# Latent attention with operands stored as two parts, softmax weights divided on ScalarE, linear attention scaled out of PSUM

## The chip, the core and the metric

One core of a Trainium2 chip runs the whole program. Its engines are TensorE (PE, with its weight loads PEld), VectorE (DVE), ScalarE (ACT), GpSimd (POOL), and SyncE (SP), which here only issues DMAs. The metric is device microseconds for one execution, from the first to the last instruction and a little around it; lower is better.

## The reference, cut to what matters

The model has two layers on a sequence of 1024 tokens with 1024 features. The change lies in the mixer of the first layer, which feeds two heads' groups from one projection:

```
q  = rmsnorm(c_q, g_q) @ w_uq          # 8 heads of 64 + 32 rotary features
kv = rmsnorm(c_kv, g_kv) @ w_ukv       # 8 heads of 64 key + 64 value features
s  = (q_nope . k_nope + rope(q_pe) . rope(k_pe)) * 96 ** -0.5, causal
a  = softmax(s) @ v                    # latent attention, f32
o  = linear attention(gq, gk, gv, decay)        # 4 heads, chunks of the sequence
g  = rmsnorm(o, g_gla) * silu(r)
mix = concat(a, g) @ w_out
```

All of it is f32. A product of two f32 operands is made on TensorE from rounded parts: x = hi + lo, and hi.hi + hi.lo + lo.hi are three matmuls into the same PSUM bank.

## The kernel before, in words

A tile framework records the program and orders each engine's instructions by its own estimate; semaphores are set by it. Within an engine the order is then fixed. Four pools matter here. `u` has 34 buffers of 4 KB a partition for nearly everything in SBUF; `t2` has 3 buffers of 128x512; PSUM has `p1` with 4 banks and `p2` with 2 buffers of two banks. A tile waits for the last reader of the buffer's former tile, and that reader can be a store to DRAM. Each DMA of the SP queue counts on one of eight semaphores in turn (DMAHW0 to 7) and waits for the former DMA on its semaphore, so that at most eight are under way.

`split` (L134 to L143) makes the two parts: ACT copies x to hi with rounding (L137), DVE subtracts hi from x for lo (L143; POOL where `lo_eng` says so). `acc3` (L145 to L151) issues the three matmuls.

`mix0` (from L881) goes through these stages, with the microseconds of the trace:

- 14 to 205: input projections, gates, the latents and their norms; then for two groups of four heads the up-projection. `uq` makes rotary and plain queries, `uk` keys, the loop over `V` values. ACT copies queries and values out of PSUM (L1207, L1220, L1234), DVE copies keys (L1223). DVE multiplies the rotary queries by cosine and sine (L1210, L1211), POOL adds (L1212). The results go to DRAM by head as f32: `mq`, `mk`, `mkr`, `mv`.
- 205 to 250: the gate r of the linear attention, eight token blocks `tok` (L1151 to L1153) of 24 matmuls each. `silu` (L393 to L400) takes each out of PSUM with DVE, three passes on ACT, DVE; POOL multiplies by the gain `ggla` (L1245), and SP stores it to `grd` (L1246). With three `t2` buffers, a block's silu needs the store of the block two before it.
- 258 to 587: 32 steps, eight heads by four row pairs, in a hand-written order. In each step `scores` (L1276) multiplies queries by keys, DVE takes the row maximum (L1302), ACT the exponential with its sum (L1304), DVE the reciprocal (L1305) and the division of the weights (L1306). `values` of two steps before and `turn` of the step before follow: `turn` transposes the weights on PE (L1319) and splits them. Every fourth step `head_qk` loads the next head's query and key to a raw tile and splits them into parts, 96x1024 each; every eighth `pair_v` does that for two heads' values. Between the steps run the linear attention `gla` (L930), one chunk of 128 tokens after the other, and `mem_side`, which prepares the cross attention and whose POOL splits (L143) read two 128x1024 tiles.
- `gla` makes decay factors `lev` (POOL L961, ACT L962, DVE L963), products `gr` on PE (L927, L976) that DVE copies under a mask (L977), and the chunk's output `o`, which sits in a `p2` buffer. ACT squares `o` (L1036), DVE multiplies `o` by the gate (L1037) and sums the squares (L1038), POOL makes the reciprocal root `stg` (L187, L188), DVE scales the four heads (L1042), PE transposes (L1048).

Of the kernel before, what the change touches and what calls it, by code (L numbers as in the profile page):

```python
# [7 lines left out]
F32 = mybir.dt.float32  # L8
# [7 lines left out]
P = 128  # L16
# [61 lines left out]
class Trunk:  # L78
# [802 lines left out]
    def mix0(self):  # L881
# [10 lines left out]
        wg, reset = c0[:, 0:256], c0[:, 256:384]  # L892
        ggla = self.cp.tile([P, P], F32, name="ggla")
        nc.sync.dma_start(ggla, self.bcast_row(T["g_gla"]))
        ones = self.cp.tile([P, P], F32, name="ones")
# [4 lines left out]

        qd, kd = self.dram("mq", [8, 96, S]), self.dram("mk", [8, 64, S])
        krd, vd = self.dram("mkr", [32, S]), self.dram("mv", [4, P, NT, P])

# [6 lines left out]
        def heads(x):  # L910
            return x.rearrange("p r (a b) -> p r a b", b=P)

        def natural(x):

            return x.rearrange("p (a r b) -> p r a b", a=2, b=P)

# [13 lines left out]
        def gla():  # L930
# [6 lines left out]
            for c in range(NT):  # L937
# [98 lines left out]
                nc.scalar.activation(at, o[:, :, 0:256], AF.Square, scale=128.0 ** -0.5)  # L1036
                nc.vector.tensor_tensor(natural(oc), heads(o[:, :, 0:256]), natural(srg), ALU.mult)  # L1037
                nc.vector.tensor_reduce(stt[:, 0:4], at.rearrange("p r (a b) -> p (r a) b", b=P), AX.X, ALU.add)  # L1038
                self.rstd(stt[:, 4:8], stt[:, 0:4])
                for hd in range(4):  # L1040
                    w, x = slice(hd * P, (hd + 1) * P), 4 + 2 * (hd % 2) + hd // 2
                    nc.vector.tensor_scalar(oc[:, w], oc[:, w], stt[:, x:x + 1], None, ALU.mult)  # L1042

                def turn(c=c, oc=oc):
                    tp = self.p1("gT")
                    for hd in range(4):
                        w = slice(hd * P, (hd + 1) * P)
                        nc.tensor.transpose(tp[:, w], oc[:, w], self.ident)  # L1048
# [13 lines left out]
        def head_qk(hd):  # L1062
            res = []
            for a in range(2):
                t = self.raw([P, S], "qk")
                if a:
                    nc.sync.dma_start(t[0:64, :], kd[hd])
                    nc.sync.dma_start(t[64:96, :], krd)
                else:
                    nc.sync.dma_start(t[0:96, :], qd[hd])  # L1070
                h, l = self.parts([96, S], "kq"[1 - a])
                self.split(h, l, t[0:96, :])
                res.append((h, l))
            qk[hd] = res

        def pair_v(pair):
            t = self.raw([P, NT, P], "V")
            nc.sync.dma_start(t.rearrange("p a b -> p (a b)"), vd[pair].rearrange("p a b -> p (a b)"))

            V[pair] = [self.u([P, NT, 2, 64], F32R, "V") for _ in range(2)]  # L1080
            for b, x in enumerate(V[pair]):
                self.split(x[:, :, 0, :], x[:, :, 1, :], t[:, :, 64 * b:64 * b + 64])


        with self.psum(4, 2):
# [55 lines left out]
            nc.gpsimd.tensor_tensor(kr[0:32, :], pe[0:32, :], kr[0:32, :], ALU.add)  # L1141
            nc.sync.dma_start(krd, kr[0:32, :])
            del pe, kr, wg, reset, c0

# [51 lines left out]
            for grp in range(2):  # L1196
                wuq = self.fetch(T["w_uq"][grp])

                def uq(t, half):
                    ps = self.p1("uq")  # L1200
                    self.acc3(ps, [(tuple(w[:, t * 256 + k * P:t * 256 + k * P + P] for w in wuq), tuple(x[:, half_cols(half)] for x in qn[k])) for k in range(2)])
                    return ps


                x, y = self.u([P, S], F32, "qpe"), self.u([P, S], F32, "swap")
                for half in range(2):
                    nc.scalar.activation(x[:, half_cols(half)], uq(0, half), AF.Copy, scale=asc)  # L1207
# [5 lines left out]
                for h in range(4):  # L1213
                    nc.sync.dma_start(qd[4 * grp + h, 64:96, :], x[32 * h:32 * h + 32, :])
                for pair in range(2 * grp, 2 * grp + 2):
                    q, k = self.u([P, S], F32, "q"), self.u([P, S], F32, "k")
                    w = slice(pair * P, pair * P + P)
                    for half in range(2):
                        c = half_cols(half)
                        nc.scalar.activation(q[:, c], uq(1 + pair % 2, half), AF.Copy, scale=asc)  # L1220
# [3 lines left out]
                    for b in range(2):  # L1224
                        nc.sync.dma_start(qd[2 * pair + b, 0:64, :], q[64 * b:64 * b + 64, :])
                        nc.sync.dma_start(kd[2 * pair + b], k[64 * b:64 * b + 64, :])
                w = slice(512 + grp * 256, 512 + grp * 256 + 256)
                for i in range(NT):
                    if not i % 4:
                        v = self.u([P, 4, 2, P], F32, "v")  # L1230
# [3 lines left out]
                    nc.scalar.activation(v[:, i % 4], ps[:, :256].rearrange("p (a b) -> p a b", a=2), AF.Copy)  # L1234
                    if i % 4 == 3:
                        for a in range(2):
                            nc.sync.dma_start(vd[2 * grp + a][:, i - 3:i + 1, :], v[:, :, a, :])
            del wuq, wkv, qn, kn, x, y, q, k, v, cs, sn
            self.rope = None
            wv = [W.next() for _ in range(4)]  # L1240
            for i in range(NT):
                x = self.t2()
                self.silu(x, tok(i, wv), self.t2())
                v = x.rearrange("p (a b) -> p a b", b=P)
# [8 lines left out]
            del wv, x, v  # L1253
        self.hn = [None, None]
# [10 lines left out]
        with self.psum(4, 2):  # L1265
# [10 lines left out]
            def scores(hd, r):  # L1276
# [3 lines left out]
                for a in range(2):  # L1280
# [24 lines left out]
                    nc.vector.reciprocal(st[:, 3:4], st[:, 2:3])  # L1305
                    nc.vector.tensor_scalar(p, p, st[:, 3:4], None, ALU.mult)  # L1306
                    pts.append(p)
                probs[hd, r] = pts

            def turn(hd, r):  # L1310
# [3 lines left out]
                for jp in range(r + 1):  # L1314
# [3 lines left out]
                    for n, (jj, a) in enumerate(cells):  # L1318
                        nc.tensor.transpose(tp[:, n * P:n * P + P], pts[a][:, (2 * jp + jj) * P:(2 * jp + jj + 1) * P], self.ident)  # L1319
                    x = self.u([P, 2, 512], F32R, "pTs")  # L1320
# [6 lines left out]
            def values(hd, r):  # L1327
                xs = probs.pop((hd, r))
                b, pair = hd % 2, hd // 2
                v = V[pair][b]  # L1330
                po = self.p1("pv")
                n = 2 * r + 2
                for j in range(n):
# [3 lines left out]
                    for a in ((0, 1) if j < n - 1 else (1, 0)):  # L1337
                        if a:
                            mm(po[0:64, :256], v[:, j, 0, :], x[:, 1, c], start=False, stop=False)
                        else:  # L1340
                            mm(po[:, :256], v[:, j].rearrange("p a b -> p (a b)"), x[:, 0, c], start=j == 0, stop=j == n - 1)
                o = self.t2()
# [6 lines left out]
            for n, (hd, r) in enumerate(seq):  # L1349
                if r == 2 and hd < 7:  # L1350
                    head_qk(hd + 1)
                if n % 8 == 1:
                    pair_v(hd // 2)
                scores(hd, r)
                if r == 3:
# [14 lines left out]
            wo = [self.fetch(T["w_out0"][k]) for k in range(4)]  # L1370
            values(*seq[-2])
            turn(*seq[-1])
            self.side(0)
# [450 lines left out]
def pack(inputs):  # L1824
# [52 lines left out]
    A["g_q"], A["g_kv"] = cols(f["ev_g_q"][0]), cols(f["ev_g_kv"][0])  # L1877
    A["g_gla"] = f["ev_g_gla"]
    A["w_out0"] = km(f["ev_w_out"][0])
# [61 lines left out]
```

## Time and profile before

| | |
|---|---|
| median of three runs | 2979.53 us (2977.46 to 2980.94) |
| the profiled execution | 2979.67 us |
| its span, first to last instruction | 2977.9 us |
| PE busy | 2846.6 us, 96% of the span |
| DVE, ACT, POOL busy | 1909.4, 1402.7, 898.2 us |
| DMA | 385.09 MB, 129 GB/s over the span |
| mean granted clock of TensorE | 0.980 |

The profiled execution is 0.14 us above the median, so sums can be made against either; what lies around its span is 1.8 us. Busy time is the union of an engine's instructions. PEclk is the share of its full clock that TensorE was granted. An "idle before" or a wait names the engine or DMA that released the waiting instruction last.

### The profile page before, as it was taken

The numbers are of one execution on the slowest core, as the hardware profiler recorded it, in microseconds if no ns is written. First come the engines' busy times: TensorE is split into PE (matmuls) and PEld (weight loads), VectorE is DVE, ScalarE is ACT, GpSimd is POOL, SyncE is SP. The second block draws the span as 40 slices with busy tenths as digits, with TensorE's granted clock in tenths as the row PEclk, the third lists the DMA queues.
The fourth block names the chain that finished last, engine by engine and source line by source line (L and its number), as shares of the span: only waits on it lengthen the run. The fifth ranks groups of instructions, "written<-read, shape, count | busy, mean of one in ns | idle before, by whom it ended". The sixth has DMA issues, their size and how long they took to land. (4 is left out here: it accounts for less than half of the span.)

```text
span 2977.9 us, 37928 instructions
## 1 busy us (share of the span) xinstructions
PE 2846.6 (96%) x14470; PEld 2355.4 (79%) x14470; DVE 1909.4 (64%) x2348; ACT 1402.7 (47%) x2391; POOL 898.2 (30%) x674
## 2 busy tenths in 40 slices
PE   7998999999999999999999999889999999999998
PEld 6777888888887888787867888887788788878776
DVE  4237788754347443799876657887733744458995
ACT  4346666633346455433445565543433655544332
POOL 2204545233330000167050113357533100006723
PEclk9998999999999999999999999999999999999999
DMA  4264544352322333531163345547323233263204
GB/s 160 97 165 147 168 141 148 116 197 71 109 104 90 109 113 136 203 114 64 52 223 96 122 144 178 189 163 251 113 63 121 85 108 112 103 231 111 98 17 142
DMA packets 165222, 385.09 MB, mean 129 GB/s; under 512 B 16748, under 2 KB 66316, under 8 KB 165040
## 3 DMA queue, kind: packets, MB, share of 16 engines
q1 hardware_dynamic: 146608, 349.10, 35.0%
q10 hardware_dynamic: 18432, 33.56, 2.9%
q8 instruction: 114, 1.87, 0.3%
q14 instruction: 68, 0.56, 0.1%
HBM read 267.86 MB, written 113.69 MB: 128 GB/s over the span
## 5 line engine op out<-in xcount | busy, mean ns | idle before, releaser
L143 DVE TENSOR_TENSOR wl<-blk,wh 128x1024 fp32r<-128x1024 f32 x276 | 451.7, 1659 | 320.0 <-ACT wh L137 320.0
L493 POOL TENSOR_TENSOR blk<-blk 128x1024 f32<-128x1024 f32 x80 | 252.4, 3183 | 869.0 <-DVE wl L143 863.5
L137 ACT ACTIVATE wh<-blk 128x1024 fp32r<-128x1024 f32 x276 | 281.8, 1054 | 327.6 <-PE op L561 188.7
L560 PE MATMUL up<-hnh,wh 128*128 128x512 f32 x896 | 356.0, 398 | 9.6 <-ACT hnh L137 5.0
L561 PE MATMUL up<-hnl,wh 128*128 128x512 f32 x896 | 354.5, 396 | 4.8 <-DVE hnl L143 4.8
L562 PE MATMUL up<-hnh,wl 128*128 128x512 f32 x896 | 353.4, 395 | 0.0
L561 PE MATMUL op<-wl,wh 128*128 128x512 f32 x784 | 307.9, 393 | 9.7 <-DVE wl L143 9.6
L560 PE MATMUL op<-wh 128*128 128x512 f32 x784 | 306.3, 395 | 6.2 <-ACT wh L137 6.2
L562 PE MATMUL op<-wh,wl 128*128 128x512 f32 x784 | 306.0, 390 | 0.0
L137 ACT ACTIVATE wh<-raw 128x1024 fp32r<-128x1024 f32 (+1 forms) x163 | 170.6, 1058 | 138.1 <-DMA raw<-hd 25.9
L143 POOL TENSOR_TENSOR wl<-raw,wh 128x1024 fp32r<-128x1024 f32 x66 | 158.9, 2420 | 223.6 <-ACT wh L137 208.3
L560 PEld LDWEIGHTS up<-hnh,wh 128*128 128x128 f32 x896 | 169.1, 189 | 51.3 <-ACT hnh L137 11.4
L561 PEld LDWEIGHTS up<-hnl,wh 128*128 128x128 f32 x896 | 169.3, 189 | 45.5 <-DVE hnl L143 6.3
L562 PEld LDWEIGHTS up<-hnh,wl 128*128 128x128 f32 x896 | 169.3, 189 | 40.1
L143 DVE TENSOR_TENSOR wl<-raw,wh 128x1024 fp32r<-128x1024 f32 (+1 forms) x97 | 126.6, 1315 | 99.7 <-ACT wh L137 99.3
L561 PEld LDWEIGHTS op<-wl,wh 128*128 128x128 f32 x784 | 148.0, 189 | 47.1 <-DVE wl L143 16.4
L560 PEld LDWEIGHTS op<-wh 128*128 128x128 f32 x784 | 149.1, 191 | 39.0 <-ACT wh L137 8.2
L562 PEld LDWEIGHTS op<-wh,wl 128*128 128x128 f32 x784 | 147.8, 188 | 30.5
L187 POOL TENSOR_SCALAR st<-st 128x1 f32<-128x1 f32 x99 | 41.6, 421 | 361.6 <-ACT hn L303 307.4
L306 POOL TENSOR_TENSOR h<-h,hn 128x1024 f32<-128x1024 f32 x47 | 128.4, 2732 | 33.5 <-DVE hn L305 26.2
L673 DVE TENSOR_TENSOR acc<-acc,op 128x512 f32<-128x512 f32 x192 | 123.8, 676 | 4.3 <-PE op L562 4.1
L287 DVE SCALAR_TENSOR_TENSOR hn<-h,st,gain 128x1024 f32<-128x1024 f32 x48 | 101.8, 2122 | 26.1 <-POOL st L188 24.8
(440 smaller groups left out, 6993.5 us busy)
## 6 DMA issues: line engine op xcount, KB each, us to landing
blk<-in_ffn_w_dram SPq DMA_DIRECT2D x120, 512.0 KB, 4.3
h<-h SPq DMA_DIRECT2D x80, 512.0 KB, 4.1
hd<-t ACTq DMA_DIRECT2D x128, 256.0 KB, 2.9
blk<-hd SPq DMA_DIRECT2D x56, 512.0 KB, 4.2
raw<-in_w_in_dram SPq DMA_DIRECT2D x24, 512.0 KB, 4.1
h<-in_x_dram SPq DMA_DIRECT2D x16, 512.0 KB, 6.3
raw<-in_xa_w_k_dram SPq DMA_DIRECT2D x16, 512.0 KB, 3.7
raw<-in_xa_w_v_dram SPq DMA_DIRECT2D x16, 512.0 KB, 3.8
```

Source lines behind the costliest of these rows:

```text
L137: nc.scalar.activation(hi, src, AF.Copy)
L143: e.tensor_tensor(lo, src, hi.bitcast(F32), ALU.subtract)
L187: self.nc.gpsimd.tensor_scalar(dst, src, EPS, None, ALU.add)
L287: nc.vector.scalar_tensor_tensor(hn, h, st[:, 1:2], gpre, ALU.mult, ALU.mult)
L306: nc.gpsimd.tensor_tensor(h, h, t, ALU.add)
L493: eng.tensor_tensor(out, a, b, op)
L560: mm(ps, lh, rh, start=start and not i, stop=False, skip_group_check=True)
L561: mm(ps, lh, rl, start=False, stop=False, skip_group_check=True)
L562: mm(ps, ll, rh, start=False, stop=i == n - 1, skip_group_check=True)
L673: nc.vector.tensor_tensor(dst, dst, ps[i], ALU.add)
```

## The change

- Queries, keys and rotary keys are split where they leave PSUM, and both parts go to DRAM (`mq`, `mk`, `mkr` get an axis of two); `head_qk` loads parts straight into `u` tiles. Query and key tiles now hold half of the tokens with both parts. Values are split likewise, in tiles of two token blocks, and `pair_v` loads them.
- The rotary queries are made after the group's values, all three passes on POOL; ACT takes the high part, POOL the low one.
- The weights are no longer divided on DVE in `scores` but by ACT, in `divide`, called one step later, ahead of the next `scores`.
- In `gla` the product of `o` and the gate and the scaling are one DVE operation for each head, which reads `o` from PSUM once `stg` is there. The gain `g_gla` is applied as a scale of the copy after the transpose, and POOL's multiplication by `ggla` is gone.

```diff
-                nc.vector.tensor_tensor(natural(oc), heads(o[:, :, 0:256]), natural(srg), ALU.mult)
                 nc.vector.tensor_reduce(stt[:, 0:4], at.rearrange("p r (a b) -> p (r a) b", b=P), AX.X, ALU.add)
                 self.rstd(stt[:, 4:8], stt[:, 0:4])
                 for hd in range(4):
-                    nc.vector.tensor_scalar(oc[:, w], oc[:, w], stt[:, x:x + 1], None, ALU.mult)
+                    nc.vector.scalar_tensor_tensor(oc[:, w], o[:, a, p * P:p * P + P], stt[:, x:x + 1], srg[:, w], ALU.mult, ALU.mult)
...
-                    nc.scalar.activation(g, tp, AF.Copy)
+                    nc.scalar.activation(g, tp, AF.Copy, scale=ggla)
...
-                h, l = self.parts([96, S], "kq"[1 - a])
-                self.split(h, l, t[0:96, :])
+                for part, t in enumerate(res[a]):
+                    if a:
+                        nc.sync.dma_start(t[0:64, :].bitcast(F32), kd[hd, part])
+                        nc.sync.dma_start(t[64:96, :].bitcast(F32), krd[part])
+                    else:
+                        nc.sync.dma_start(t.bitcast(F32), qd[hd, part])
...
-                nc.vector.tensor_tensor(x, x, cs, ALU.mult)
-                nc.vector.tensor_tensor(y, y, sn, ALU.mult)
-                nc.gpsimd.tensor_tensor(x, x, y, ALU.add)
...
+                        q, k = self.u([P, 2, HALF], F32R, "q"), self.u([P, 2, HALF], F32R, "k")
+                        ps = uq(1 + pair % 2, half)
+                        nc.scalar.activation(q[:, 0], ps, AF.Copy, scale=asc)
+                        nc.vector.scalar_tensor_tensor(q[:, 1], ps, asc, q[:, 0].bitcast(F32), ALU.mult, ALU.subtract)
...
-                        nc.vector.tensor_copy(k[:, c], ps)
+                        self.split(k[:, 0], k[:, 1], ps)
+                        for b in range(2):
+                            for t, dst in ((q, qd), (k, kd)):
+                                nc.sync.dma_start(dst[2 * pair + b, :, 0:64, c].rearrange("r p t -> p r t"), t[64 * b:64 * b + 64].bitcast(F32))
...
+                nc.gpsimd.tensor_tensor(x, x, cs, ALU.mult)
+                nc.gpsimd.tensor_tensor(y, y, sn, ALU.mult)
+                nc.gpsimd.tensor_tensor(x, x, y, ALU.add)
+                xs = self.parts([P, S], "qpe")
+                self.split(*xs, x, lo_eng="pool")
...
-                nc.gpsimd.tensor_tensor(v, v, ggla.unsqueeze(1).broadcast_to([P, 4, P]), ALU.mult)
...
-                    nc.vector.tensor_scalar(p, p, st[:, 3:4], None, ALU.mult)
+            def divide(hd, r):
+                for p, st in probs[hd, r]:
+                    nc.scalar.activation(p, p, AF.Copy, scale=st[:, 3:4])
```

The first place is the SP queue at the end of the up-projection. `mq`, `mk`, `mv` are the stores of queries, keys and values, `qpe` the rotary queries, `grd` the first store of the gate r, and `qk` the load of head 0. Before:

```order
L1225 DMA mq<-q 64x1024
L1226 DMA mk<-k 64x1024
L1237 DMA mv<-v 128x4x128 x2
L1214 DMA mq<-qpe 32x1024 x4
L1237 DMA mv<-v 128x4x128 x2
L1070 DMA qk<-mq 96x1024
```

Now, at the same place:

```order
L1218 DMA mq<-q 64x2x512
L1218 DMA mk<-k 64x2x512
L1230 DMA mv<-v 128x2x256 x8
L1238 DMA mq<-qpeh 32x1024 x4
L1238 DMA mq<-qpel 32x1024 x4
L1246 DMA grd<-t_1736 128x512
L1067 DMA qh<-mq 96x1024
L1067 DMA ql<-mq 96x1024
```

The stores of both parts, twice as many bytes, now stand ahead of the first gate store and of head 0's load, and the rotary queries come last.

The second place is ACT in the second group's up-projection, with the semaphores that each row waits for; `q` and `k` are new tiles, which take the buffers of stored ones. Now:

```order
L1211 ACTIVATE q_1628<-uq_1630 128x512 [waits DMAHW1_49,DMAHW2_49,DMAHW0_49,DMAHW3_49,PE_49,Pool_49]
L137 ACTIVATE k_1629<-uk_1639 128x512 [waits DMAHW6_49,DMAHW5_49,DMAHW7_49,DMAHW4_49,PE_49]
L137 ACTIVATE v_1649<-V_1650 128x4x64 [waits PE_49]
...
L137 ACTIVATE qpeh_1712<-qpe_1539 128x1024 [waits Activation_49,Pool_49]
L397 ACTIVATE t2_1762<-t2_1762 128x512 [waits DVE_49]
```

The last query and key tile of group 2 wait for four DMAs each: these are the stores of group 1's `qpeh` and `qpel` (four DMAs each, on DMAHW0 to 3 and 4 to 7), whose buffers they take over. The values (`v`) follow, and the rotary part of group 2 stands ahead of the first silu (L397).

The third place is DVE in the linear attention of chunk 0, `o` being the chunk's output in PSUM, `t_2235` or `t_2304` its SBUF tile, and `stg` the reciprocal root from POOL. Before, the product stands first (L1037, a few rows up, with the sum L1038 behind it); the scaling comes here:

```order
L1302 TENSOR_REDUCE sta<-sc 128x1
L1305 RECIPROCAL sta<-sta 128x1
L1306 TENSOR_SCALAR prob<-prob,sta 128x896
L1305 RECIPROCAL sta<-sta 128x1
L1306 TENSOR_SCALAR prob<-prob,sta 128x1024
L143 TENSOR_TENSOR pTs<-pT,pTs 128x512 x2
L143 TENSOR_TENSOR pTs<-pT,pTs 128x384
L1042 TENSOR_SCALAR t_2235<-t_2235,stg 128x128 x4
```

Now:

```order
L1033 TENSOR_REDUCE stg<-at 128x4
L1030 COPY gS<-su 128x128 x2
L977 TENSOR_TENSOR at<-gr,c_ident 128x512
L143 TENSOR_TENSOR mtl<-tp,mth 128x4x128 x3
L959 TENSOR_TENSOR lev<-lev,G 128x256 x3
L1302 TENSOR_REDUCE sta<-sc 128x1
L959 TENSOR_TENSOR lev<-lev,G 128x256
L1038 SCALAR_TENSOR_TENSOR t_2304<-o,stg,vr 128x128 x4
L1305 RECIPROCAL sta<-sta 128x1
L1348 TENSOR_TENSOR t_2365<-pv,t_2365 64x256
L1302 TENSOR_REDUCE sta<-sc 128x1
```

The divisions are gone from DVE, and `o` is read only at L1038, behind `stg`, with a reciprocal and a row maximum queued behind it.

More of the change, by code (lines that the diff above doesn't have):

```diff
@@ L892, in mix0 @@
         wg, reset = c0[:, 0:256], c0[:, 256:384]
-        ggla = self.cp.tile([P, P], F32, name="ggla")
-        nc.sync.dma_start(ggla, self.bcast_row(T["g_gla"]))
+        ggla = self.const("g_gla")
         ones = self.cp.tile([P, P], F32, name="ones")
@@ L1064, in head_qk @@
             for a in range(2):
[L1065 to L1070, printed above, removed]
-                h, l = self.parts([96, S], "kq"[1 - a])
-                self.split(h, l, t[0:96, :])
-                res.append((h, l))
+                res.append(self.parts([96, S], "kq"[1 - a]))
+                for part, t in enumerate(res[a]):
[4 more added lines that the diff above has]
+                        nc.sync.dma_start(t.bitcast(F32), qd[hd, part])
             qk[hd] = res
         def pair_v(pair):
[L1077 to L1082, printed above, removed]
+            V[pair] = [self.u([P, 4, 2, 2, 64], F32R, "V") for _ in range(2)]
+            for t, src in zip(V[pair], vd[pair]):
+                nc.sync.dma_start(t.rearrange("p a b c d -> p (a b c d)").bitcast(F32), src.rearrange("p a b c d -> p (a b c d)"))
         with self.psum(4, 2):
@@ L1141, in mix0 @@
             nc.gpsimd.tensor_tensor(kr[0:32, :], pe[0:32, :], kr[0:32, :], ALU.add)
-            nc.sync.dma_start(krd, kr[0:32, :])
-            del pe, kr, wg, reset, c0
+            krs = self.parts([32, S], "kr")
+            self.split(*krs, kr[0:32, :])
+            for part, t in enumerate(krs):
+                nc.sync.dma_start(krd[part], t.bitcast(F32))
+            del pe, kr, krs, wg, reset, c0
             def tok(i, ws):
@@ L1219, in mix0 @@
                         c = half_cols(half)
-                        nc.scalar.activation(q[:, c], uq(1 + pair % 2, half), AF.Copy, scale=asc)
+                        q, k = self.u([P, 2, HALF], F32R, "q"), self.u([P, 2, HALF], F32R, "k")
+                        ps = uq(1 + pair % 2, half)
+                        nc.scalar.activation(q[:, 0], ps, AF.Copy, scale=asc)
+                        nc.vector.scalar_tensor_tensor(q[:, 1], ps, asc, q[:, 0].bitcast(F32), ALU.mult, ALU.subtract)
                         ps = self.p1("uk")
                         self.acc3(ps, [(tuple(x[:, w] for x in wkv), tuple(x[:, c] for x in kn))])
-                        nc.vector.tensor_copy(k[:, c], ps)
-                    for b in range(2):
-                        nc.sync.dma_start(qd[2 * pair + b, 0:64, :], q[64 * b:64 * b + 64, :])
-                        nc.sync.dma_start(kd[2 * pair + b], k[64 * b:64 * b + 64, :])
+                        self.split(k[:, 0], k[:, 1], ps)
+                        for b in range(2):
+                            for t, dst in ((q, qd), (k, kd)):
+                                nc.sync.dma_start(dst[2 * pair + b, :, 0:64, c].rearrange("r p t -> p r t"), t[64 * b:64 * b + 64].bitcast(F32))
+                del q, k
                 w = slice(512 + grp * 256, 512 + grp * 256 + 256)
                 for i in range(NT):
-                    if not i % 4:
-                        v = self.u([P, 4, 2, P], F32, "v")
+                    if not i % 2:
+                        v = self.u([P, 2, 2, 2, 2, 64], F32R, "v")
                     ps = self.p1("V")
@@ L1233, in mix0 @@
                     self.acc3(ps[:, :256], [(tuple(x[:, t] for x in kn), tuple(x[:, w] for x in wkv))])
-                    nc.scalar.activation(v[:, i % 4], ps[:, :256].rearrange("p (a b) -> p a b", a=2), AF.Copy)
-                    if i % 4 == 3:
+                    self.split(v[:, i % 2, :, :, 0, :], v[:, i % 2, :, :, 1, :], ps[:, :256].rearrange("p (a b c) -> p a b c", a=2, b=2))
+                    if i % 2:
                         for a in range(2):
-                            nc.sync.dma_start(vd[2 * grp + a][:, i - 3:i + 1, :], v[:, :, a, :])
-            del wuq, wkv, qn, kn, x, y, q, k, v, cs, sn
+                            nc.sync.dma_start(vd[2 * grp + a, i // 4][:, i % 4 - 1:i % 4 + 1].rearrange("p i b r c -> p i (b r c)"), v[:, :, a].rearrange("p i b r c -> p i (b r c)").bitcast(F32))
+                nc.gpsimd.tensor_tensor(x, x, cs, ALU.mult)
[3 more added lines that the diff above has]
+                self.split(*xs, x, lo_eng="pool")
+                for part, t in enumerate(xs):
+                    for h in range(4):
+                        nc.sync.dma_start(qd[4 * grp + h, part, 64:96, :], t[32 * h:32 * h + 32, :].bitcast(F32))
+                del x, y, xs, t
+            del wuq, wkv, qn, kn, v, cs, sn
             self.rope = None
@@ L1252, in mix0 @@
                     next(linear)
-            del wv, x, v
+            del wv, x
         self.hn = [None, None]
@@ L1329, in values @@
                 b, pair = hd % 2, hd // 2
-                v = V[pair][b]
+                v = [t[:, j, b] for t in V[pair] for j in range(4)]
                 po = self.p1("pv")
@@ L1353, in mix0 @@
                     pair_v(hd // 2)
+                if n:
+                    divide(*seq[n - 1])
                 scores(hd, r)
@@ L1371, in mix0 @@
             values(*seq[-2])
+            divide(*seq[-1])
             turn(*seq[-1])
@@ L1877, in pack @@
     A["g_q"], A["g_kv"] = cols(f["ev_g_q"][0]), cols(f["ev_g_kv"][0])
-    A["g_gla"] = f["ev_g_gla"]
+    A["g_gla"] = cols(f["ev_g_gla"][0])
     A["w_out0"] = km(f["ev_w_out"][0])
```

21 lines of the change are left out of this document (8 added, 13 removed).

## The prediction

> **What bounds the kernel now.** The change touches only the first mixer, so I read the busy time of its stages first (microseconds, busy time and instructions of PE, PEld, DVE, ACT, POOL, the granted clock, DMA share, GB/s): the gate's stage, and that of the 32 attention steps.
>
> ```profile
> core 0: us, PE busy (x) PEld busy (x) DVE busy (x) ACT busy (x) POOL busy (x), PEclk, DMA share, GB/s
> 206.00:251.00 45.00, 45.00 (x204) 35.88 (x202) 20.87 (x28) 17.86 (x31) 15.39 (x18) 1.00 0.74 221
> 258.00:587.00 329.00, 307.47 (x2529) 274.65 (x2527) 264.15 (x484) 206.24 (x422) 143.66 (x151) 0.95 0.43 138
> ```
>
> In the gate's stage PE has no gap and its full clock. In the steps PE is idle for 329 - 307.5 = 21.5 us, and a clock of 0.95 costs about 0.05 x 329 = 16.5 us. So 38 us is all that any relief of other engines can give here. DVE is the busiest of them, 264 of 329 us. PE's waits in that stage say what the gaps wait for (us in total, times, longest):
>
> ```profile
> PE gr L927 <- ACT prob L1304: 7.1, 3, 3.2
> PE gr L927 <- DVE lev L963: 4.1, 1, 4.1
> PE gT L1048 <- DVE t L1344: 2.9, 3, 1.4
> PE sc L1296 <- DVE pTs L143: 1.6, 2, 1.0
> PE gT L1048 <- DVE t L1042: 1.5, 1, 1.5
> PE vo L149 <- DVE t L1344: 1.2, 1, 1.2
> PE pT L1319 <- DVE prob L1306: 1.0, 1, 1.0
> ```
>
> The first row names ACT, but one such gap, in order of time, shows DVE behind it:
>
> ```profile
> 364.36 0.69 DVE L1037 TENSOR_TENSOR t<-o,vr 128x512 f32<-128x512 f32 x1 [1.29 <-ACT at L1036]
> ...
> 369.06 1.04 POOL L188 TENSOR_TENSOR stg<-stg,mhalf 128x4 f32<-128x4 f32 x1
> ...
> 372.02 4.71 POOL L143 TENSOR_TENSOR wl<-raw,wh 128x1024 fp32r<-128x1024 f32 x2 [1.92 <-ACT wh L137]
> 372.31 4.81 DVE L1042 TENSOR_SCALAR t<-t,stg 128x128 f32<-128x128 f32 x3
> 377.04 2.20 DVE L1302 TENSOR_REDUCE sta<-sc 128x1 f32<-128x896 f32 x2
> 378.15 1.01 ACT L1304 ACTIVATE prob<-sc,sta 128x896 f32<-128x896 f32 x1 [5.27 <-DVE sta L1302]
> 379.30 0.86 PE L927 MATMUL gr<-lev 64*128 64x128 f32 x8 [3.16 <-ACT prob L1304]
> ```
>
> The scaling's three operations end just after POOL's split of a weight; the row maximum is late by that, the exponential waits 5.27 us for it, and PE 3.16 us for the exponential, which holds the PSUM buffer. How far this goes, from the two kinds of DVE operation (fastest, middle, longest in ns):
>
> ```profile
> L1042 DVE TENSOR_SCALAR t<-t,stg x32: 270/281/2635, 289.6 to 580.8; 128x128 f32<-128x128 f32 x32
> L143 DVE TENSOR_TENSOR pTs<-pT,pTs x80: 531/670/692, 267.1 to 593.2; 128x512 fp32r<-128x512 f32 x48, 128x384 fp32r<-128x384 f32 x32
> ```
>
> The operation between SBUF tiles goes from 281 to 2635 ns where POOL works on SBUF; the one with a PSUM operand has no outlier in 80. [...] Behind such gaps the clock is low too:
>
> ```profile
> 379.00:384.00 5.00, 4.59 (x73) 4.03 (x74) 4.47 (x11) 4.10 (x11) 0.00 (x0) 0.66 0.30 91
> 427.00:435.00 8.00, 7.47 (x89) 6.70 (x90) 6.64 (x16) 5.38 (x14) 0.81 (x2) 0.57 0.30 90
> 471.00:476.00 5.00, 5.00 (x28) 4.62 (x27) 3.85 (x10) 2.09 (x6) 1.34 (x3) 0.66 0.31 116
> 550.00:558.00 8.00, 7.02 (x41) 6.57 (x42) 5.71 (x14) 3.99 (x12) 0.00 (x0) 0.57 0.12 42
> ```
>
> Their loss is 0.34 x 5 + 0.43 x 8 + 0.34 x 5 + 0.43 x 8 = 10.3 us of the 16.5.
>
> **The change part by part: the steps.** What leaves and stays, by groups (busy us, mean ns of one | idle before):
>
> ```profile
> L1306 DVE TENSOR_SCALAR prob<-prob,sta 128x256 f32<-128x256 f32 (+3 forms) x64 | 51.2, 810 | 1.3
> L143 DVE TENSOR_TENSOR ql<-qk,qh 96x1024 fp32r<-96x1024 f32 x7 | 8.5, 1217 | 1.0 <-ACT qh L137 1.0
> L143 DVE TENSOR_TENSOR kl<-qk,kh 96x1024 fp32r<-96x1024 f32 x7 | 8.5, 1215 | 0.0
> L143 DVE TENSOR_TENSOR V<-V 128x512 fp32r<-128x512 f32 x8 | 5.7, 728 | 0.2 <-ACT V L137 0.2
> L1037 DVE TENSOR_TENSOR t<-o,vr 128x512 f32<-128x512 f32 x8 | 5.5, 682 | 3.5 <-ACT at L1036 3.5
> L1032 DVE SCALAR_TENSOR_TENSOR gS<-gS,ekq,su 128x128 f32<-128x128 f32 x12 | 3.6, 342 | 3.8 <-PE su L1028 3.8
> ...
> L137 ACT ACTIVATE qh<-qk 96x1024 fp32r<-96x1024 f32 x7 | 7.3, 1048 | 0.0
> L137 ACT ACTIVATE kh<-qk 96x1024 fp32r<-96x1024 f32 x7 | 7.3, 1047 | 0.0
> L137 ACT ACTIVATE V<-V 128x512 fp32r<-128x512 f32 x8 | 4.6, 628 | 0.0
> ...
> L962 ACT ACTIVATE lev<-lev 128x256 f32<-128x256 f32 x49 | 18.8, 422 | 8.8 <-POOL lev L961 8.8
> L137 ACT ACTIVATE wh<-raw 128x1024 fp32r<-128x1024 f32 x39 | 41.0, 1058 | 5.2 <-DMA raw<-in_w_out_dram 5.1
> ```
>
> DVE loses 51.2 (divisions), 8.5 + 8.5 + 5.7 (splits) and 5.5 (the product), and its 32 scalings, 9 us unblocked, become 32 products from PSUM. That form isn't in the trace: between 281 ns, as before, and 342 ns, the nearest with three operands; I take 342, 10.9 us. DVE falls by some 77 to 85 us, to about 182 of 329.
>
> ACT gains 64 divisions. From 422 ns for 256 columns and 1058 for 1024, one costs 210 ns and 0.83 ns a column; a head's eight rows of weights have 4736 columns together, so 5.6 us a head and 45 us in all. The splits give back 7.3 + 7.3 + 4.6 = 19.2. ACT ends near 206 + 26 = 232 of 329, under DVE's share of before. The division is issued one step after its exponential, ahead of the next exponentials; it stands up to 1.06 us each in their way, and the weights' transposes wait for it. That is covered while a step on PE (329 / 32 = 10.3 us) is longer than ACT's 232 / 32 = 7.2; uncovered, two divisions a step would cost up to 2 us each time.
>
> What goes of PE's 38 us: the waits quoted, all but the 4.1 us behind `lev` (two SBUF inputs on DVE, beside POOL, unchanged), make 15.3 us, and the clock behind such gaps 10.3. That is 25. Late next is `o`: its PSUM buffer was free of the product at 365.05 and waits now for `stg`, 370.1 in the timeline, some 5 us later in a pool of two buffers that scores and `gr` use too. And L1038 waits for POOL with reciprocals and row maxima queued behind it. Eight chunks by 5 us would be 40, but a buffer is asked for only in part of that; I charge 5 us, a sixth or so, and take a gain of **20 us**, between 12 and 25.
>
> **The stores.** DVE's and ACT's added splits of the projection run beside PE and get no price; what doubles is bytes. From the shapes, f32 queries of 8 x 96 x 1024, keys of 8 x 64 x 1024 and values of as many are 3.15 + 2.10 + 2.10 = 7.34 MB, so 14.68 now. All of it stands on SP ahead of the first gate store. Before, first store, rates at hand, and the end of the gate's last block:
>
> ```profile
> 184.97 0.54 SPq L1225 DMA_DIRECT2D mq<-q  x1
> ```
>
> ```profile
> 180.00:185.00 5.00, 5.00 (x23) 4.04 (x22) 1.38 (x2) 1.79 (x3) 0.00 (x0) 1.00 0.49 84
> 206.00:214.00 8.00, 8.00 (x36) 6.46 (x35) 3.71 (x4) 1.90 (x3) 2.40 (x1) 1.00 0.95 243
> 225.00:229.00 4.00, 4.00 (x18) 3.21 (x18) 2.78 (x3) 3.01 (x4) 0.00 (x0) 1.00 1.04 386
> ```
>
> ```profile
> 254.67 0.69 DVE L396 TENSOR_SCALAR t<-tok 128x512 f32<-128x512 f32 x1
> ...
> 257.39 0.69 DVE L400 TENSOR_TENSOR t<-tok,t 128x512 f32<-128x512 f32 x1 [1.38 <-ACT t L399]
> ```
>
> At 243 GB/s, the rate of stores back to back (DMA share 0.95), 14.68 MB take 60.4 us and end at 245.4. Small pieces in 180 to 185 ran at 84 GB/s for a share of 0.49, so 171 if alone; large ones in 225 to 229 at 386. Those are the bounds, and I take 243, the same kind of transfer. The first gate store lands some 2 us later; the third block's silu waits for it, as its `t2` buffer is that store's source. Then six blocks follow, one after the other on DVE and ACT, 258.08 - 254.67 = 3.4 us each: 20.4. With 2 us for the decay passes between them, an estimate, the last ends at 269.9 instead of 258.08: PE, which now does without a gap, stands still and the scores begin **12 us** later. At 386 it is about 3 (the values end later anyhow, their tiles waiting for group 1's stores), at 171 it is 37. Gain and loss are equal at 253.6 for the stores' end, 214 GB/s.
>
> [...]
>
> **The sum.** 2979.67 + 12 - 20 = 2971.7, rounded to 2971.5. The profiled execution is 0.14 us above the median, so it needs no correction. Nothing behind 600 us is charged, since there PE's order is as before.
>
> **The rivals.**
> 1. *The stores drain slower than the gains pay for* (slower). Twice as many pieces, of half the length, go nearer to 171 than to 243: at 190 GB/s they end at 262.3, the lag is 28.7, and the time 2979.67 + 28.7 - 20 = 2988.4. It decides below 214 GB/s. For it: PE's gapless 206 to 251, where any delay shows. Against it: 243 with pieces of 64 partitions. 0.22.
> 2. *The relief of DVE turns into a wait for `o` or for ACT* (no change). The `p2` buffers are held until POOL's root, and ACT's divisions stand ahead of exponentials. Gain 12, lag 12: 2979.7. For it: POOL is in front of DVE in order, and waits 1.92 us for ACT even in the rows above. Against it: ACT at 70%. 0.25.
> 3. *The backlog is hidden*: transfers overlap as in 225 to 229, lag 3, so 2962.7. Against it: those were loads, not stores. 0.13.
>
> That leaves 0.40 for the forecast, whose own range is 2964 to 2979. Both signs hold much of the chance, so the range goes from the third case with its full gain (2979.67 + 0 - 25 = 2955) to beyond the first (2992); the first and second together, 2996, are left out. A measurement of this kernel can tell about 0.2%, 6 us. Faster: 0.85 of the forecast's 0.40 and the third, 0.47. Same: 0.06 of the forecast and 0.17 of the second, 0.23. Slower: the first and 0.08 of the second, 0.30.
>
> **What would show it.** Right: last gate store's block near 270 and PE idle some 12 us between 239 and 270; in the steps DVE near 182 and ACT near 232 us, no L1038 over 0.5 us, PE's wait for L1304 below 3 us and a granted clock near 0.98 there. Wrong: scores begin before 262 or after 280; PE waits for `p2` behind L1038, or for divisions on ACT; or the clock stays at 0.95, so that the gaps had another cause.

## The result, and the profile after

The changed kernel takes 2997.99 us (median of 4 runs, 2996.52 to 3001.72), beside 2980.24 for the kernel before in the same set (4 runs). The ratio is 1.0062, 95% interval 1.0044 to 1.0079: some 18 us slower, where 8 us faster were forecast. The profiled execution is the fastest of the four, 2996.52 us with a span of 2994.1.

Where the time went is read from lags: the start of the same matmul in both traces, counted along each product's name, after minus before. The last column is the same for a second pair of traces, `changed_again` and `before_again`.

| place (us in the trace of before) | lag of the changed kernel, us | second pair, us |
|---|---|---|
| first up-projection (176) | -3.3 | 0.7 |
| gate's stage begins (205) | 11.5 | 15.8 |
| first score (258) | 16.0 | 18.7 |
| ninth matmul of the output projection (590) | 5.5 | 17.0 |
| second layer begins (1522) | 9.0 | 14.8 |
| its output projection (2022) | 16.7 | 24.5 |
| end | 16.2 | 24.2 |

So the start is 16 us late in the first pair, 19.3 counted from the lead of 3.3 us that this trace had at 176, and 18.0 in the second pair. The attention steps give back 10.5 us in the first pair and only 1.7 in the second. A stretch that the change doesn't touch then takes 10.7 and 7.2 us. The stages of the changed kernel, with the columns of the table of before (the steps now lie at 274 to 600):

```profile
core 0: us, PE busy (x) PEld busy (x) DVE busy (x) ACT busy (x) POOL busy (x), PEclk, DMA share, GB/s
...
206.00:251.00 45.00, 40.07 (x171) 32.06 (x169) 10.03 (x18) 12.39 (x24) 10.30 (x6) 0.92 0.87 235
```

```profile
274.00:600.00 326.00, 309.01 (x2570) 275.60 (x2568) 197.59 (x399) 239.42 (x474) 137.40 (x149) 0.97 0.56 169
```

The window of the gate's stage, gapless before, now has 5 us without PE work and a clock of 0.92; these gaps are, but for 0.5 us, the up-projection's last, as its `V` matmuls now run to 216. In the steps DVE went from 264 to 198 us and ACT from 206 to 239, close to the 182 and 232 forecast. But PE is still idle for 326 - 309 = 17 us, against 21.5. Its waits there:

```profile
PE sc L1296 <- DVE pTs L143: 4.2, 4, 1.6
PE sc L1296 <- ACT prob L1304: 3.0, 1, 3.0
PE pv L1345 <- ACT pTs L137: 1.8, 1, 1.8
PE gT L1044 <- DVE t L1038: 1.8, 1, 1.8
```

The waits behind exponentials went from 7.1 to 3.0, and the 4.1 behind `lev` is gone; others grew or came anew: the split of transposed weights (`pTs`, 1.6 before, 4.2 now), and in the last step `values`, which waits for ACT's part of that split. The start, on SP's queue and then on DVE:

```profile
181.83 0.67 SPq L1218 DMA_DIRECT2D mq<-q  x1
...
240.94 1.95 SPq L1238 DMA_DIRECT2D mq<-qpel  x4
243.01 0.35 SPq L1246 DMA_DIRECT2D grd<-t  x1
...
246.25 0.54 SPq L1246 DMA_DIRECT2D grd<-t  x1
```

```profile
245.85 0.69 DVE L400 TENSOR_TENSOR t<-tok,t 128x512 f32<-128x512 f32 x1 [11.31 <-DMA grd<-t]
253.94 0.69 DVE L396 TENSOR_SCALAR t<-tok 128x512 f32<-128x512 f32 x1 [7.39 <-DMA grd<-t]
...
274.11 0.69 DVE L400 TENSOR_TENSOR t<-tok,t 128x512 f32<-128x512 f32 x1 [1.17 <-ACT t L399]
```

The first gate store is issued at 243.0, behind the last rotary store. The third block's silu waits 11.31 us for it, the fourth 7.39 us for the second one, and the eighth ends at 274.8; before, that was 258.1. The first score starts at 274.2. PE's own waits ahead of it are these: in the changed kernel the three that make 3 us or more between 176 and the first score, in the kernel before all of them:

```profile
PE gr L923 <- DMA G<-gld: 5.1, 1, 5.1
PE V L149 <- DVE q L1212: 4.7, 3, 3.2
...
PE V L149 <- DVE k L143: 3.0, 2, 2.3
```

```profile
PE gr L927 <- ACT t L397: 4.1, 1, 4.1
PE V L149 <- DVE k L1223: 0.6, 1, 0.6
```

In the up-projection PE waits nine times for splits, 9.6 us in all, and loses 6.8 us in two half-clock stretches that before doesn't have. ACT, which makes the high parts, waits there 13.7 us for stores whose buffers it needs. Then PE waits 5.1 us for the load `G`. Its last wait before the first score is 0.92 us. So in this trace PE arrives at the scores late by itself, at about the time at which the silus end.

### The profile page after: what moved, and what is told of

Read it like the earlier page. It is cut to its first block, busy times and chain, and to the rows that moved or that the text cites. A ratio compares the mean times of both kernels' runs of the same rounds, so it can differ in the third digit from the quotient of the medians.

```text
span 2994.1 us, 38042 instructions
## 1 busy us (share of the span) xinstructions
PE 2850.7 (95%) x14470; PEld 2357.7 (79%) x14470; DVE 1840.9 (61%) x2273; ACT 1435.0 (48%) x2442; POOL 895.7 (30%) x672
```

## The experiments

Three theories were on trial. A: the doubled stores delay the start. B: relieving VectorE of divisions and scaling is worth some 20 us in the steps. C: what is lost in the second layer is clock, not code. D came later: VectorE's busy time is not the cost; the cost is that some of its operations between SBUF tiles take longer beside GpSimd's splits (a scaling in before 2635 ns at worst, 281 in the middle), which the expectations call the lock. For each run, PE's idle time in the steps (gaps between matmuls, from the first score to the ninth matmul of the output projection) and the clock loss there (half of each stretch of half the clock that begins there) are worked out from its trace; decay is the mean of one `lev<-lev,G` on DVE in that stage.

| kernel | ratio to before, 95% interval | median us | first score | PE idle | clock loss | decay ns |
|---|---|---|---|---|---|---|
| before (two traces) | | 2979 | 258.2, 256.9 | 21.5, 22.4 | 15.4, 11.9 | 545 |
| changed (two traces) | 1.0062, 1.0044 to 1.0079 | 2997.99 | 274.2, 275.6 | 17.0, 17.3 | 8.5, 15.4 | 626 |
| parts_only | 1.0086, 1.0071 to 1.0101 | 3004.73 | 278.1 | 18.6 | 15.4 | 628 |
| divide_and_scale | 0.9991, 0.9981 to 1.0000 | 2976.47 | 253.2 | 18.0 | 6.8 | 793 |
| divide_only | 1.0061, 1.0045 to 1.0077 | 2996.53 | 256.6 | 31.4 | 20.5 | 712 |
| scale_only | 1.0035, 1.0022 to 1.0048 | 2989.54 | 252.5 | 24.6 | 17.1 | 569 |
| gate_between | 1.0077, 1.0063 to 1.0091 | 2997.84 | 257.1 | 32.4 | 20.5 | 686 |
| high_part_only | 1.0008, 0.9998 to 1.0019 | 2978.71 | 258.9 | 19.9 | 15.4 | 652 |
| values_whole | 1.0068, 1.0054 to 1.0082 | 2994.46 | 276.7 | 17.5 | 10.2 | 627 |
| gate_on_act_queue | 1.0063, 1.0047 to 1.0080 | 2997.31 | 280.6 | 15.0 | 10.2 | 625 |
| changed_splits_dve | 1.0072, 1.0059 to 1.0085 | 2999.84 | 278.5 | 15.2 | 11.9 | 461 |
| divide_splits_dve | 1.0009, 0.9999 to 1.0018 | 2981.86 | 258.1 | 20.2 | 6.8 | 461 |
| splits_dve_only | 0.9972, 0.9960 to 0.9985 | 2971.21 | 256.5 | 16.3 | 8.5 | 469 |
| divide_scale_splits_dve | 0.9965, 0.9951 to 0.9978 | 2968.08 | 256.6 | 13.8 | 6.8 | 450 |

The median of before was 2976.4 to 2980.2 in these sets; the ratio is against the runs beside each.

**Parts alone.** Of the change's diff only the stores, the source splits and the loads of parts; in this kernel the product of `o` and the gate takes the heads in another order than the reference (same instructions).

> The kernel before with only the stores in parts (queries, keys, rotary keys and values split where they leave PSUM, rotary queries after the values on GpSimd); the division stays on VectorE and the linear attention is scaled as before. Theory A (the doubled stores cost the start of the attention steps): the first score comes near 274 us as in the changed kernel, against 258 before. Theory B (the gain in the steps comes from the divisions and the scaling that left VectorE): the steps give back at most 6 of these 16 us here, so about 2990 us. Rival to B (it is the 23 us of splits that left VectorE): the steps give back 12 or more, about 2983. In both cases up to 10 us more may come in the second layer.

The first score came at 278.1, and the steps gave back 1.7 us (lag 19.9 at the first score, 18.2 at the output projection); 26 us slower in all, where 11 were expected. The late start of theory A is there, and the 23 us of splits that left VectorE bring nearly nothing alone.

**The other two parts, together and each alone.**

```diff
-                    nc.vector.tensor_scalar(p, p, st[:, 3:4], None, ALU.mult)
+            def divide(hd, r):
+                for p, st in probs[hd, r]:
+                    nc.scalar.activation(p, p, AF.Copy, scale=st[:, 3:4])
```

> The kernel before with only the division on ScalarE and the linear attention scaled out of PSUM; stores as before. Theories A and B: the first score stays at 258 us, PE is ahead of the kernel before by 10 to 16 us at the last attention step and keeps 5 to 10 of it into the output projection, so 2965 to 2975. Rival to A (the start is late because of VectorE's or ScalarE's work on the gate, not the stores): the start is late here too. Rival to B: no gain in the steps, 2980.

> The kernel before with only the division on ScalarE, one step later. Theory B with the division as the larger part (51 us leave VectorE, 45 come to ScalarE): PE ahead by 8 to 12 us at the last step, minus some 3 to 5 us given back in the last steps, where the division stands alone in the chain: 2973. Rival (the tail alone costs as much as the division brings): 2980 to 2983.

> The kernel before with only the linear attention's scaling out of PSUM. If the blocked scalings (12 us over their unblocked time, and PE gaps at 376 and 424 us) are the larger part: 2972. If the held PSUM buffer costs as much as the lock did: 2980, with PE waits behind L1038 in place of those behind the scaling.

Together they start on time. Idle time and clock loss of the steps make 24.8 us in the trace instead of 36.9, but counted by lag the steps gain 5.9 us, that trace is the fastest of ten runs, and the medians differ by 2.6. Alone each is slower, by 17 and 10 us: theory B, as a sum of parts, falls.

The scaling alone, out of PSUM, brought waits of the scores for `pTs` (1.6 us in before, 2.0 with the division alone), and hardly any behind its own line, which the expectation named (1.7 us):

```profile
PE sc L1293 <- DVE pTs L143: 7.6, 4, 2.9
PE sc L1293 <- ACT prob L1301: 4.2, 1, 4.2
PE wk L149 <- DVE pTs L143: 3.0, 1, 3.0
```

With the division as well they are 6.2 us, and 4.2 in the changed kernel. What makes `pTs` late there, the held `o` or another order on DVE and ACT, no run isolates.

The division alone shows what happens. DVE, POOL and a PE wait around 276 us in its trace:

```profile
276.37 6.47 DVE L963 TENSOR_TENSOR lev<-lev,G 128x256 f32<-128x256 f32 x3
282.76 2.07 DVE L1042 TENSOR_SCALAR t<-t,stg 128x128 f32<-128x128 f32 x4
284.75 1.21 DVE L1302 TENSOR_REDUCE sta<-sc 128x1 f32<-128x1024 f32 x1
```

```profile
275.19 7.36 POOL L143 TENSOR_TENSOR wl<-raw,wh 128x1024 fp32r<-128x1024 f32 x3
```

```profile
PE gr L927 <- ACT prob L1304: 13.6, 5, 3.9
PE kt L149 <- DVE t L1348: 8.6, 1, 8.6
```

Three decay products take 6.47 us beside three splits on POOL, where the middle one of 56 in before takes 0.42 us; the row maximum, the exponential and PE (8.6 us) wait behind them. Without the divisions, other operations on two SBUF tiles stand beside POOL's splits: the decay products went from 545 to 712 ns on average, the scaling from 639 to 824. DVE is busy 242 us of 350 there, less than before, and the kernel is slower. So the share of DVE's busy time was no measure here of what its relief is worth.

**Bytes or the work of splitting.** The splits stay, the low parts of queries, keys and rotary queries aren't stored, and the high parts are loaded in their place (so the products' low terms are made from high parts):

```diff
-  nc.sync.dma_start(dst[2 * pair + b, :, 0:64, c]..., t[64 * b:64 * b + 64].bitcast(F32))
+  nc.sync.dma_start(dst[2 * pair + b, 0, 0:64, c], t[64 * b:64 * b + 64, 0].bitcast(F32))
```

> The changed kernel that splits as it does but stores only the high parts of queries, keys and rotary queries (9.4 MB instead of 14.7), and loads them as both parts; the products' low parts are thus wrong. Theory A: the last store of group 2 is issued some 22 us earlier (5.3 MB at 240 GB/s), the waits of ScalarE for buffers under store shrink, first score at 258 to 264. Rival (the work of splitting): 272 to 275.

The first gate store is issued at 227.1 instead of 243.0, the first score comes at 258.9, and the kernel is level with before. With all the splitting still done, the start's lag is gone (0.8 us at the first score): it came from storing the low parts, that is from their bytes and from the transfers that carry them, which this run doesn't tell apart. ACT waits 0.9 us for stores in place of 13.7. One wait of PE behind the splits stays, 3.6 us, and the lag of 4.2 at 205 with it; the slack of 4.1 us that before had ahead of its scores takes it up. The longest wait for a gate store is 5.16 us, and the last silu ends on time:

```profile
230.22 0.69 DVE L396 TENSOR_SCALAR t<-tok 128x512 f32<-128x512 f32 x1 [5.16 <-DMA grd<-t]
...
259.07 0.69 DVE L400 TENSOR_TENSOR t<-tok,t 128x512 f32<-128x512 f32 x1 [1.39 <-ACT t L399]
```

**Fewer bytes, an earlier stage, another queue.** First the values stored whole:

> The changed kernel with the values stored whole as f32 and split when they are loaded, as before (12.6 MB instead of 14.7, and VectorE gets 6 us and ScalarE 5 us of splits back in the steps). Theory A by bytes: the first score 5 to 9 us earlier than 274, and the steps lose at most 2 us: 2990 to 2994. Rival: within 2 us of the changed kernel.

A miss: the first gate store went 4 us earlier (238.8), but the third and fourth silu still waited 10.4 and 3.8 us for stores, both memory norms stood between the others, and the first score came at 276.7; here PE did stand still for a silu, 10.2 us. Then the gate's stage between the two groups:

```diff
+                if not grp:
+                    wv = [W.next() for _ in range(4)]
+                    for i in range(NT):
+                        x = self.t2()
...
```

> The changed kernel with the gate's stage r (eight token blocks, 45 us of PE) moved between the two groups of the up-projection, so that group 1's 7.3 MB of stores drain beside PE work that needs no buffer of them, and group 2's under the first attention steps. Theory A (the start is late because 14.7 MB of stores stand ahead, in the buffers and in front of the gate's stores and the first loads): the first score comes at 258 to 264 us instead of 274, and the time falls to 2980 to 2986. Rival (the splits on VectorE and ScalarE in the projection cost the time themselves): the first score stays near 272.

The first score came at 257.1, as theory A says, and the time was the same as the changed kernel's. The cost had moved: the second chunk's load `G` now stands behind group 2's stores and is issued at 282.8, and PE waits for it:

```profile
282.84 0.37 SPq L936 DMA_DIRECT2D G<-gld  x1
```

```profile
PE gr L923 <- DMA G<-gld: 10.2, 1, 10.2
```

And the gate stores on ScalarE's queue:

```diff
-                nc.sync.dma_start(grd[i], x)
+                nc.scalar.dma_start(grd[i], x)
```

> The changed kernel with the eight gate stores issued on ScalarE's DMA queue instead of SP's, where they stood behind the 14.7 MB. Theory A2 (the third block's silu waits for the first gate store, and that chain of silus sets the first score): no wait of VectorE for a gate store over 4 us, the silus end near PE's own pace, and the first score comes at 262 to 268 us instead of 274 to 276; the projection's own stalls of PE (12 us at 205) are then what is late. Rival (stores share the same 16 engines, so the gate stores land as late from either queue): 272 or later.

The first score came at 280.6, later still, and not for the rival's reason: the store wasn't issued until 240.03. The author's reading is that it waited, as on SP's queue, for the former DMA on its semaphore; by the profile ACT's 11.63 us of idle time in front of the next silu ended with an earlier store of values:

```profile
240.03 0.34 ACTq L1246 DMA_DIRECT2D grd<-t  x1
240.43 0.63 ACT L397 ACTIVATE t<-t 128x512 f32<-128x512 f32 x1 [11.63 <-DMA mv<-v]
```

**The splits on VectorE.** The 32 low parts of the memory weights (1.22 us each on DVE, 2.4 on POOL) go to DVE:

```diff
-        W = Stream(self, blocks, 1, "pool")
+        W = Stream(self, blocks, 1, "pool" if l else "dve")
```

> The changed kernel with the low parts of the 32 memory weights of the first layer made on VectorE instead of GpSimd (39 us of 1.22 us splits on VectorE, 76 us off GpSimd). Theory D (the lock between GpSimd's splits and VectorE's operations on two SBUF tiles lengthens the decay products from 0.42 to 0.63 us, 10 us in all, and causes part of the waits that are left): the decay products average below 0.5 us, PE's idle time in the steps falls from 17 to 10 to 14 us, 2990 to 2995. Rival (VectorE's added 39 us cost more than the lock): idle time 20 or more, 3000.

> The division on ScalarE and the scaling out of PSUM, stores as before, and the same 32 splits on VectorE. Theory D: decay products from 0.79 us to below 0.5, PE's idle time in the steps from 18 to 10 to 14, and 2965 to 2972, under both kernels. Rival: VectorE, with the splits of queries and keys still on it, becomes late: 2976 or more.

> The division alone on ScalarE (17 us slower than before), with the 32 splits on VectorE as well. Theory D (the division alone loses because the decay products and the SBUF scalings now meet GpSimd's splits: 6.5 us for three decay products at 276, and PE waits of 8.6 and three times 3.8 us behind them): PE's idle time in the steps falls from 31 us to 18 to 22, decay products below 0.5 us on average, and 2974 to 2982. Rival (ScalarE's divisions in front of the exponentials cost the time): idle time stays near 30, 2992 or more.

> The kernel before with only the 32 splits on VectorE; division, scaling and stores as before. Theory D with VectorE near its limit (268 + 39 - 20 us of lock in 336): the lock goes, but VectorE is late for its own sake; idle time of PE in the steps 18 to 26, 2975 to 2985. Rival (the splits' engine is the whole gain of the fastest kernel, and division and scaling bring nothing): 2970 or less.

The decay products as groups, in before, in the changed kernel, and in the fastest (busy us, mean ns):

```profile
L963 DVE TENSOR_TENSOR lev<-lev,G 128x256 f32<-128x256 f32 x49 | 24.7, 545 | 0.8 <-ACT lev L962 0.8
```

```profile
L959 DVE TENSOR_TENSOR lev<-lev,G 128x256 f32<-128x256 f32 x49 | 28.7, 626 | 4.8 <-ACT lev L958 4.8
```

```profile
L962 DVE TENSOR_TENSOR lev<-lev,G 128x256 f32<-128x256 f32 x49 | 20.0, 450 | 3.4 <-ACT lev L961 3.4
```

In all four runs they fell to 450 to 469 ns. The division alone went from 1.0061 to 1.0009, its PE idle time from 31.4 to 20.2 us, as theory D says: the divisions' place on ScalarE, unchanged here, is not what cost most of it. The same word also takes 76 us of splits out of GpSimd's own queue, in front of its part of the decay factors; no run separates this from the longer operations on VectorE. On the kernel before, one word makes it faster by 0.28%, more than expected, though DVE then works 284 of 332 us:

```profile
258.00:590.00 332.00, 315.71 (x2599) 281.62 (x2599) 284.45 (x526) 214.87 (x435) 75.44 (x118) 0.97 0.47 148
```

The three waits of `gr` behind exponentials, 7.1 us in before, are down to this, with the scaling still on SBUF tiles, which fits the prediction's reading of them, scalings late beside GpSimd's splits (4.81 us for three at 372.31):

```profile
PE gr L927 <- ACT prob L1304: 0.8, 1, 0.8
```

With division and scaling as well it is 2968.08 us, ratio 0.9965, the fastest here; the intervals of the two overlap, so what division and scaling add to it isn't settled. In the changed kernel the same word gives nothing in time (1.0072), and idle time fell only from 17.0 to 15.2 us where 10 to 14 were expected, though the decay products fell to 461 ns: that expectation missed, and nothing shows the meeting with GpSimd's splits to be the main part of what is left idle there.

**Second traces.**

> The changed kernel once more, for a second trace. In the second layer (from 1500 us on) the two traces of before and after differ by 10 us, nearly all of it in half-clock stretches of 3.4 us behind the same waits. Theory C (these stretches fall as they do by the moment at which a wait begins, not by the code): this trace loses another amount there, between 15 and 26 us of clock. Rival (the changed kernel has waits of its own there): the same waits and 24 us within 1.

> The kernel before once more, for a second trace. Theory C: its idle time of PE in the steps is again 21 to 22 us, while the half-clock loss of the steps and of the second layer moves by several us either way (15.4 and 11.9 us in the first trace). Rival: both within 1 us.

PE's idle time in the steps came out within 1 us in each pair, the clock loss there moved by 3.5 and 6.9. From 1522 to 2022 us of before the clock loss was 11.9 and 13.7 us in the two traces of before and 20.5 and 18.8 in those of the changed kernel. That alone looks like a loss that belongs to the changed kernel. But over all sixteen traces it runs from 11.9 to 22.2 us, and not by what is stored: it is 13.7 in `parts_only`, which stores every part, and 22.2 in `divide_only` and in `divide_scale_splits_dve`, which store every operand whole; in `divide_and_scale` it is 13.7. So no part of the change goes with it, as theory C says, but what sets it isn't shown: two traces of one kernel lie within 1.8 us.

## Why the prediction was wrong

The forecast was 2971.5 us and the kernel took 2998.0. By the lags of the first pair, the start cost 4 us more than the 12 forecast (7 counted from the lead at 176), the steps brought 9.5 less than 20, and 10.7 came in the stretch behind them that was charged nothing; the other 2 us lie between the traces and the medians. Storing the low parts of queries and keys is what makes the kernel slower than before: in `high_part_only`, which does all the rest, the ratio is 1.0008.

- **The stores' rate** was right: 14.7 MB from 181.8 to 242.9 are 240 GB/s (forecast 243), and the first gate store was issued at 243.0, against 245.4.
- **The silu chain** was there, too short, and not what held PE in this trace. The sentence that failed is "the first gate store lands some 2 us later", as if the second came along: the first landed at about 245.9, but the second was issued among the loads of head 0 and landed 7.7 us after that. With two memory norms (1.27 and 1.63 us) on DVE between the silus, the last ended at 274.8, not 269.9. But PE's last wait before the first score is 0.92 us, and in front of the gate's last rows it stood for the load `G`, not for a silu. So that the 12 us forecast came near the measured 16 was luck: another chain was as long. In `parts_only`, `gate_on_act_queue` and `values_whole` PE does stand still for a silu there, 4.3, 6.2 and 10.2 us.
- **The projection's splits, priced at nothing,** are the step of the start that failed: "DVE's and ACT's added splits of the projection run beside PE and get no price". PE goes from 3.3 us ahead at 176 to 11.5 behind at 205, by 9.6 us of waits for splits (0.6 before) and 6.8 us of half clock. Most of it is the stores once more, as ACT waits for buffers under store: without the low parts' stores the lag at 205 is 4.2.
- **The gain of 20 us** is the main failure, by its step "the waits quoted, all but the 4.1 us behind `lev` ... make 15.3 us", which let them go and put nothing in their place but 5 us for `o`. Of these 15.3 us, rows of the same kind still make 10.0 (3.0 behind exponentials, 4.2 `pTs`, 1.8 behind L1038, 1.0 behind a division); the 4.1 us that was to stay is gone; and waits that the prediction didn't list went from 2.1 to 7.0 us. L1038 did what was said of it, while the decay products met the splits as before (fastest, middle, longest in ns; forecast 342, no outlier):

```profile
L1038 DVE SCALAR_TENSOR_TENSOR t<-o,stg,vr x32: 335/341/353, 298.1 to 579.9; 128x128 f32<-128x128 f32 x32
L959 DVE TENSOR_TENSOR lev<-lev,G x56: 405/423/2619, 256.8 to 556.0; 128x256 f32<-128x256 f32 x56
```

  The decay products grew longer in the scalings' place (545 to 626 ns, 793 without the stored parts). In `divide_only` PE waits 8.6 us behind them. In the changed kernel it seems the smaller part: no wait of PE there ends at a decay product, and without the splits on GpSimd, though with 39 us more work on DVE, its idle time is still 15.2 us. The largest part of what is left, 7.2 us of 17, is waits for `pTs`, whose cause stays open. The prediction's rows show a scaling between SBUF tiles go from 281 to 2635 ns where POOL works on SBUF; this should have been read for what stays on DVE too, not only for what leaves it: the decay products, between SBUF tiles as well, fell to 450 ns without the splits on POOL. PE's idle time fell by 4.5 us, not 15. The signs that the prediction set for the steps nearly all came true (DVE 198 and ACT 239 us, no L1038 over 0.353 us, 3.0 us behind L1304, a clock of 0.97): they watched the relief, and PE's idle time alone would have shown what it was worth.
- **The clock's 10 us** came as 6.9 us in the first trace and -3.5 in the second pair (11.9 before, 15.4 changed): a term that no single profile can carry.
- **`o` held in PSUM** for 5 us more showed no PE wait of its own over the 1.8 us behind L1038; whether the waits for `pTs` that came with it belong to it stays open.
- **"Nothing behind 600 us is charged"** failed by 7 to 11 us. Each engine's order there is as before but for a few rows. One piece is seen: the load of the second layer's first `v`, issued at 1783.64, reaches ACT 8.2 us later (before 1775.06, 5.6 us), ACT's silu stands behind it, and PE waits:

```profile
1780.70 1.07 ACT L137 ACTIVATE vah<-v 128x1032 fp32r<-128x1032 f32 x1 [0.98 <-DMA v<-vd]
```

```profile
1791.85 1.06 ACT L137 ACTIVATE vah<-v 128x1032 fp32r<-128x1032 f32 x1 [3.57 <-DMA v<-vd]
...
1794.88 1.12 PE L736 MATMUL tp<-c_ident,memn 128*128 128x128 f32 x4 [2.63 <-DVE sz L400]
```

With the half-clock stretch behind it that makes 4 us. It stood in all six traces of kernels that store and load every part (8.2 to 9.2 us from issue to ACT: the changed one twice, parts_only, gate_between, gate_on_act_queue, changed_splits_dve), and in none of the other ten (5.2 to 6.0). Why the load takes longer in them stays open. The rest is mostly half-clock loss behind waits that are nearly the same in both kernels; it doesn't follow what is stored, and what sets it stays open.

The slower rival (2988.4) had the right sign, but not by its own condition, a rate under 214 GB/s. The second rival's gain of 12 us was nearer to the steps (10.5 and 1.7) than the forecast's 20.

## What to carry to other kernels

An engine's busy share didn't price its relief here (VectorE from 264 to 198 us, PE's idle time from 21.5 to 17): look at what its long operations collide with, and whether what is left will collide in their place. Doubling what is stored was paid where a buffer under store is asked for again (13.7 us of ACT's waits), where the first later transfer stands behind it in the queue (the first gate store at 243.0, 221.5 before), and where a small pool of buffers waits for that transfer (11.31 us); moving the stage, or the queue, moved the wait without removing it (10.2 us for `G`, 11.63 on ACT). Before removing a load from the bottleneck, try the one-word change of which engine does the colliding work: here it brought 0.28% on the kernel before, and nothing on the changed one.

## What the runs showed of the hardware

- The half-clock stretches, the last of a trace aside, last 3.41 us or two or three times that (21 in the trace of before, 23 in that of the changed kernel) and begin on a grid of 3.413 us. Its phase against the first instruction was 0.85 us in before and 2.56 in the changed kernel. In before a stretch began at 1895.25, within a wait of 2.53 us (1892.96 to 1895.49). That wait comes five times between 1865 and 1976, 2.5 to 3.1 us long; four times a stretch begins within 0.8 us of its end, once none. One kernel's runs went from 2960.79 us at a mean clock of 0.986 to 2974.71 at 0.979 (divide_scale_splits_dve).
- A DVE product of two SBUF tiles (`lev`) went from a middle of 0.42 us to 2.6 at worst with POOL's splits (before and the changed kernel), and to 0.84 at worst without them (divide_scale_splits_dve); L1038, with an operand in PSUM, kept its time beside the splits (335 to 353 ns in 32, the changed kernel).
- A gate store on ScalarE's queue didn't pass SP's backlog: it was issued at 240.03, and ScalarE's wait of 11.63 us there ended with an earlier store of values (gate_on_act_queue).
